# Reading the scores' blocks back from DRAM: four 32-partition reads in place of one with a broadcast outermost dimension

## The chip, the cores and the metric

The kernel runs on one core of one Trainium2 chip. The metric is the device time of one execution in microseconds (us). Before the change the median of three runs is 1072.54 us (1072.24 to 1074.22).

## The reference, cut to what matters

One layer of a decoder trunk on 512 tokens with a model width of 2048. Half of the width is an RWKV-7 group of 16 heads of 64 channels, the other half a causal pooling group; both are gated, concatenated, projected and added to the residual, and a gated embedding and a last norm follow.

```python
h = rms_norm(x, norm_g[i])
z = jnp.einsum('btd,dn->btn', h, w_in[i])          # r, k, v, two loras, gates, pool input
...
kk = (k * k_k[i]).astype(f32).reshape(B, T, N_HEADS, HEAD_SIZE)
kk = kk / jnp.maximum(jnp.linalg.norm(kk, axis=-1, keepdims=True), KK_EPS)
...
def step(S, inp):                                   # the recurrence over 512 tokens
    r_t, w_t, k_t, v_t, kk_t, a_t = inp
    sa = jnp.einsum('bhvk,bhk->bhv', S, -kk_t)
    S = (S * w_t[:, :, None, :]
         + sa[..., None] * (kk_t * a_t)[:, :, None, :]
         + v_t[..., None] * k_t[:, :, None, :])
    y_t = jnp.einsum('bhvk,bhk->bhv', S, r_t)
...
x = x + jnp.einsum('btc,cd->btd', y_mix, w_out[i])
gate = jax.nn.sigmoid(jnp.einsum('btd,de->bte', x, w_pg[i]) + b_pg[i])
x = x + gate * jnp.einsum('btq,qd->btd', p[i], w_ple[i])
```

## The kernel before, in words

**Stages.** The first 60 us load and normalise x and turn it. From there to about 715 us the RWKV heads run, two heads (128 channels) at a time, in eight blocks j = 0 to 7, while the large projections of `w_in` fill the gaps on TensorE. The rest are the output projection and the gate (`acc_o`, `acc_g`). All large products are done in three float32 parts: `mm3` (L167) multiplies the high part of the weights by the high and low part of the activations, and the low part by the high one.

**Weights.** `wsplit` (L127) loads a 256 KB chunk (`raw`, issued by SP), makes its rounded part on ScalarE (`whi`, L132) and the rest on VectorE (`wlo`, L133). Each of `raw`, `whi` and `wlo` has four buffers, so a chunk's `whi` can only be made when TensorE has finished with the chunk four before it, and a `raw` load is issued when the `wlo` four before it is made.

**A block.** The recurrence is done in chunks of 64 tokens. `prepare` makes the scaled keys and queries; `scores` (L646) multiplies them on TensorE (`pm`), masks the products into `mt` on VectorE (L661), writes the 32x32 diagonal parts to DRAM as `nd` (L677, four writes), and reads them back (L682) into two tiles `n_0` and `n_1` of 128 partitions (the name `n` in the trace), in which each of four groups of 32 partitions holds the same copy. `invert` (L702) inverts the small triangular blocks in 31 steps on VectorE, two instructions each: `tm` (L709), then `xw` (L713). The first 16 steps read `n_0`, the other 15 `n_1`. The result goes to DRAM (`xd`, L717) and back (`x1`, L724; its name in the trace is `x`), and `gather` (L730) turns it (`y`, L777), multiplies it on TensorE (`pq`) and prepares the next recurrence.

**The recurrence.** `recur(j)` (L812) goes through eight chunks: TensorE `py`, VectorE `zs` (L844), TensorE `pu`, ScalarE copies of `pu` (L858), TensorE `ps`, VectorE `sbd` (L874). Between these steps `pump` puts groups of matmuls of the large projections (`zg`, `zk`, `zr`, `zv`, `zb`). The inversion of block j+1 is done during the recurrence of block j, and so are the first steps on the keys of block j+2: `prepare_key` (L559) squares the key on ScalarE into `kk` (L562), splits it into `kqh` (ScalarE, L140) and `kql` (VectorE, L141); `norm_key` (L568) sums both with two matmuls named `pss` on TensorE, at a fixed place after the fifth chunk. The tile `kk` has the same buffer as `n_0`.

**What sets the order.** From the RWKV stage on (`pin`, L348) TensorE keeps the order of the program. On the other engines and on the queue of SP, a scheduler puts the instructions into a fixed order when the kernel is built, by its own estimate of durations; `issue_after` and `high_priority` move some of them. On the chip each engine then takes its instructions strictly in that order, so an instruction that waits holds up all that stand behind it on the same engine.

Of the kernel before, what the change touches and what calls it, by code (L numbers as in the profile page):

```python
# [34 lines left out]
def trunk_kernel(ctx: ExitStack, tc: tile.TileContext, x, p, norm_g, w_in, mu, w0, w_up, a0, a_up,  # L35
                 k_k, k_a, r_k, ln_w, ln_b, w_pool, pool_scale, w_out, w_ple, w_pg, b_pg, final_g, out):
    nc = tc.nc
    PSUM = bass.MemoryType.PSUM
    x, p, w_in, w_out, w_ple, w_pg = x[0], p[0, 0], w_in[0], w_out[0], w_ple[0], w_pg[0]
    out = out[0]  # L40
# [118 lines left out]
    def mm(*a, **k):  # L159
        i = nc.tensor.matmul(*a, **k)  # L160
        return tc.keep_in_program_order(i) if pin[0] else i
# [34 lines left out]
    n_ = 0  # L196
# [13 lines left out]
    for kind, nm, j in jobs:  # L210
# [7 lines left out]
        else:  # L218
            g, i = j // 4, j % 2
# [79 lines left out]
    for d in range(KT):  # L299
        xt_half(0, d)  # L300
        if d in WPOS:
            c = len(wl_)
# [18 lines left out]
    for g, win in enumerate(WINDOWS):  # L321
        t_ = cst.tile([P, win], F32, name=f"rc{g}")
# [28 lines left out]
    def load_ab(j):  # L351
        jc = slice(j * P, (j + 1) * P)
        w2 = []
        for nm, src in (("u", w_up), ("a", a_up)):
            raw = rw.tile([P, P], F32, name=f"{nm}r{j}", tag=f"l{nm}r")
            for h in range(2):
                nc.sync.dma_start(out=raw[64 * h:64 * h + 64, :], in_=src[0, :, jc])
            w2.append((raw, rw.tile([P, P], F32R, name=f"{nm}s{j}", tag=f"l{nm}s")))
        wab[j] = w2
# [24 lines left out]
    for nm, rows in (("u", slice(0, 64)), ("a", slice(64, 128))):  # L384
# [3 lines left out]
        t_ = rw.tile([P, T], F32R, name=f"{nm}hh")  # L388
# [257 lines left out]
    def scores(j):  # L646
        ar, bk, v_ = (st_[j][n_] for n_ in ("ar", "bk", "v_"))
        kph, kpl = st_[j].pop("kp")

        mt = rw.tile([P, 2, 8, 2, C], F32, name=f"mt{j}", tag="mt", bufs=2)  # L650
        pm = [[psM.tile([P, T], F32, name=f"pm{j}_{par}0", tag="m"),
               psY.tile([P, T], F32, name=f"pm{j}_{par}1", tag="y")] for par in range(2)]
        for par in range(2):
            for q in range(4):
                for h in range(2):
                    rows = slice(64 * h, 64 * h + 64)
                    mm(pm[par][h][:, q * P:(q + 1) * P], bk[rows, q, 2 * par:2 * par + 2, :],
                       ar[rows, q, 2 * par:2 * par + 2, :], start=True, stop=True)
        for par in range(2):
            for h in range(2):  # L660
                nc.vector.tensor_tensor(mt[:, par, h::2, :, :],  # L661
                                        pm[par][h].rearrange("p (u a t) -> p u a t", u=4, a=2),
                                        msk[:, par:par + 2, :].unsqueeze(1).to_broadcast([P, 4, 2, C]), ALU.mult)


        ps = psM.tile([P, T], F32, name=f"pbo{j}", tag="m")
        mm(ps, blk, kph, start=True, stop=False)
        mm(ps, blk, kpl, start=False, stop=True)
        bv = rw.tile([P, T], F32, name=f"bv{j}", tag="bv", bufs=2)
        nc.vector.tensor_tensor(bv, ps, v_, ALU.mult)  # L670

        nd = dram.tile([2, 2, 8, 32, 32], F32, name=f"nd{j}", tag="nd")
        for par in range(2):
            pb = 64 * (1 - par)
            for b in range(2):
                rows = slice(pb + 32 * b, pb + 32 * b + 32)
                nc.sync.dma_start(out=nd[par, b].rearrange("u r c -> r u c"),  # L677
                                  in_=mt[rows, par, :, 1 - par, 32 * b:32 * b + 32])
        nb = []
        for i in range(2):  # L680
            t_ = rw.tile([P, 16, 32], F32, name=f"n32{j}_{i}", tag=("kk", "kp")[i])
            n_ = nc.sync.dma_start(out=t_, in_=nd[:, :, :, 16 * i:16 * i + 16, :].rearrange(  # L682
                "a b u r c -> (a b u) r c").unsqueeze(0).to_broadcast([4, 32, 16, 32]))
            nb.append(t_)
        if j + 1 < NJ:
            with tc.issue_after(n_.ins):
                load_ab(j + 1)
        bg = rw.tile([P, NCH, 4, 32], F32, name=f"bg{j}", tag="bk")
        with tc.issue_after(n_.ins):
            for q in range(4):  # L690
                nc.sync.dma_start(out=bg[32 * q:32 * q + 32],
                                  in_=st_[j]["bkd"].rearrange("(b k) (c q i) -> q k c b i", b=4, q=4, i=32)[q])
        if j:
            vg, vd = vgs[j]
            with tc.issue_after(n_.ins):
                for q in range(4):
                    nc.sync.dma_start(out=vg[32 * q:32 * q + 32],
                                      in_=vd.rearrange("(b k) (c q i) -> q k c b i", b=4, q=4, i=32)[q])
        st_[j].update(mt=mt, nb=nb, bv=bv, bg=bg)
# [260 lines left out]
    prepare(0)  # L960
    pump(H3)
    scores(0)
    pump(H2)
    for _ in invert(0):
# [3 lines left out]
    for j in range(NJ):  # L968
        def between():
            pump(H3 if j + 1 < NJ else HC[2])  # L970
            if j + 1 < NJ:
                scores(j + 1)
                pump_to(H2)

        if j + 1 == NJ:
            pn.append(rw.tile([P, 2, T // 32, 32], F32, name="pn", tag="ar", bufs=2))
            for q in range(4):
                for c in range(2):
                    nc.sync.dma_start(out=pn[0][32 * q:32 * q + 32, c],
                                      in_=p[:, c * P + 32 * q:c * P + 32 * q + 32].rearrange("(b k) i -> k b i", k=32))  # L980
        if j + 1 < NJ:
            prepare(j + 1)
        elif gates:
            gates.pop()()
        recur(j, invert(j + 1) if j + 1 < NJ else iter(()), between)
        if j + 1 < NJ:
            gather(j + 1)
# [86 lines left out]
    for ec in range(D // EC):  # L1074
# [3 lines left out]
        for tt in range(NT):  # L1078
            rows = slice(tt * P, (tt + 1) * P)
            t_ = pp.tile([P, EC], F32, name=f"x2_{ec}_{tt}", tag=("u", "sw")[tt // 2])  # L1080
# [3 lines left out]
                                in_=t_.rearrange("p (c e) -> p c e", e=P))  # L1084
# [204 lines left out]
```

## Time and profile before

| what | value |
|---|---|
| median of 3 runs | 1072.54 us (1072.24 to 1074.22) |
| the profiled execution's own time | 1077.76 us |
| its span, first to last instruction | 1076.0 us |
| granted TensorE clock, mean | 0.997 |
| TensorE (PE) busy | 1047.7 us (97%) |
| VectorE (DVE) busy | 711.7 us (66%) |
| ScalarE (ACT) busy | 435.0 us (40%) |
| DMA, mean over the span | 144 GB/s |
| reads of `nd` (n<-nd) | 16, 256 KB each |

The profile is one execution; times within it are microseconds from its first instruction. The timeline's rows give the start, the length, the engine, the line, the operation with its output and inputs, how many instructions are merged into the row, and in brackets how long the engine had been idle before it and what ended that. The order of the rows on one engine is the order in which it executes them. The view of waits adds such idle times up: total, times, longest. SPq is the queue of SyncE, from which most transfers are issued.

### The profile page before, as it was taken

To read this page: it belongs to the slowest core of one execution; us is meant where nothing else is said; L and a number is where in the kernel's file an instruction comes from. 1 tells how busy PE (TensorE), PEld (TensorE's weight loads), DVE (VectorE), ACT (ScalarE), POOL (GpSimd) and SP (SyncE) were. 2 spreads that over 40 slices of the span, in tenths; PEclk is the share of its full clock that TensorE was granted. 3 is DMA by queue.
4 is the path that set the end of the run, shared out by engine and by line. 5 is a ranking of instruction groups with operands and counts; after the bars stand their busy time and mean duration, and the time that the engine had idled before them with its cause. 6 is when DMAs were issued, how large, how long until landed. Compare 5 with 4: busy or idle time off the path is not lost.

```text
span 1076.0 us, 17131 instructions
## 1 busy us (share of the span) xinstructions
PE 1047.7 (97%) x5912; PEld 864.6 (80%) x5912; DVE 711.7 (66%) x1879; ACT 435.0 (40%) x893; POOL 72.6 (7%) x180
## 2 busy tenths in 40 slices
PE   5999999999999999999999999999999999999996
PEld 4888878888877887888888788888888888888885
DVE  6676968878688689687786977464353344435356
ACT  7633424434334345253443344544232232324337
POOL 2100011010110110101101201000000000000000
PEclk9999999999999999999999999999999999999998
DMA  7434453453443544534544453775747659454534
GB/s 237 110 115 101 135 132 95 130 139 99 143 116 100 160 105 128 128 95 133 132 118 133 112 130 108 225 259 163 183 152 190 163 145 272 129 177 159 173 98 157
DMA packets 272733, 155.41 MB, mean 144 GB/s; under 512 B 114449, under 2 KB 235386, under 8 KB 272646
## 3 DMA queue, kind: packets, MB, share of 16 engines
q1 hardware_dynamic: 244630, 125.74, 42.2%
q10 hardware_dynamic: 28016, 28.58, 8.8%
q8 instruction: 46, 0.75, 0.3%
q14 instruction: 41, 0.34, 0.1%
HBM read 128.79 MB, written 24.95 MB: 143 GB/s over the span
## 4 chain that ended last, share of the span: by engine, by line
PE 81%; DVE 9%; DMA 5%; ACT 2%; issue 2%; SPq 1%; ACTq 0%; DVEq 0%
PE acc_o L160 16%; PE acc_g L160 16%; PE zb L160 10%; PE zv L160 7%; PE zr L160 7%; PE zg L160 6%; PE zk L160 6%; PE py L160 2%; PE pple L160 2%; DMA n<-nd 1%; PE pu L160 1%; PE pm L160 1%; DMA x<-xd 1%; PE pp L160 1%; PE ps L160 1%
## 5 line engine op out<-in xcount | busy, mean ns | idle before, releaser
L133 DVE TENSOR_TENSOR wlo_g<-raw_g,whi_g 128x512 fp32r<-128x512 f32 x84 | 57.1, 687 | 76.0 <-ACT whi_g L132 73.8
L160 PE MATMUL zb<-hhi,whi_b 128*128 128x512 f32 x256 | 105.5, 412 | 0.0
L160 PE MATMUL zb<-hhi,wlo_b 128*128 128x512 f32 x256 | 100.4, 392 | 0.0
L160 PE MATMUL zb<-hlo,whi_b 128*128 128x512 f32 x256 | 99.8, 390 | 0.0
L160 PE MATMUL acc_o<-wlo_o,yhi 128*128 128x512 f32 x256 | 99.6, 389 | 0.0
L160 PE MATMUL acc_o<-whi_o,ylo 128*128 128x512 f32 x256 | 99.6, 389 | 0.0
L133 DVE TENSOR_TENSOR wlo_o<-raw_o,whi_o 128x512 fp32r<-128x512 f32 x64 | 43.9, 690 | 81.0 <-ACT whi_o L132 72.8
L160 PE MATMUL acc_o<-whi_o,yhi 128*128 128x512 f32 x256 | 94.7, 389 | 0.0
L132 ACT CAST whi_g<-raw_g 128x512 fp32r<-128x512 f32 x84 | 51.9, 620 | 103.0 <-PE acc_g L160 57.4
L160 PE MATMUL acc_g<-whi_g,x2hi 128*128 128x512 f32 x208 | 81.1, 390 | 0.0
L160 PE MATMUL acc_g<-wlo_g,x2hi 128*128 128x512 f32 x208 | 81.0, 389 | 0.0
L160 PE MATMUL acc_g<-whi_g,x2lo 128*128 128x512 f32 x208 | 80.7, 390 | 0.0
L881 POOL TENSOR_SCALAR s0p<-sbd,pw 64x64 f32<-64x64 f32 x96 | 56.4, 587 | 336.6 <-DVE sbd L874 245.1
L132 ACT CAST whi_o<-raw_o 128x512 fp32r<-128x512 f32 x64 | 39.5, 621 | 96.1 <-PE acc_o L160 55.0
L132 ACT CAST whi_b<-raw_b 128x512 fp32r<-128x512 f32 x64 | 39.6, 620 | 75.9 <-PE zb L160 22.4
L713 DVE TENSOR_TENSOR xw<-xw,tm 128x60 f32<-128x60 f32 (+24 forms) x248 | 52.2, 210 | 7.1
L160 PEld LDWEIGHTS zb<-hhi,wlo_b 128*128 128x128 f32 x256 | 48.0, 188 | 10.8
L160 PEld LDWEIGHTS acc_o<-whi_o,ylo 128*128 128x128 f32 x256 | 48.1, 188 | 10.1
L160 PEld LDWEIGHTS acc_o<-whi_o,yhi 128*128 128x128 f32 x256 | 48.0, 188 | 10.0
L160 PEld LDWEIGHTS acc_o<-wlo_o,yhi 128*128 128x128 f32 x256 | 48.0, 188 | 9.9
L133 DVE TENSOR_TENSOR wlo_b<-raw_b,whi_b 128x512 fp32r<-128x512 f32 x64 | 43.7, 684 | 17.8 <-ACT whi_b L132 17.2
L160 PEld LDWEIGHTS zb<-hhi,whi_b 128*128 128x128 f32 x256 | 48.2, 188 | 8.6
(289 smaller groups left out, 2502.2 us busy)
## 6 DMA issues: line engine op xcount, KB each, us to landing
raw_b<-in_w_in_dram SPq DMA_DIRECT2D x64, 256.0 KB
raw_o<-in_w_out_dram SPq DMA_DIRECT2D x64, 256.0 KB
raw_g<-in_w_pg_dram SPq DMA_DIRECT2D x64, 256.0 KB
raw_k<-in_w_in_dram SPq DMA_DIRECT2D x32, 256.0 KB
raw_r<-in_w_in_dram SPq DMA_DIRECT2D x32, 256.0 KB
raw_v<-in_w_in_dram SPq DMA_DIRECT2D x32, 256.0 KB
raw_g<-in_w_in_dram SPq DMA_DIRECT2D x32, 256.0 KB
bkd<-bk SPq DMA_DIRECT2D x8, 512.0 KB
```

Of the source, the lines that this page charges most:

```text
L132: made.append(nc.scalar.copy(hi, raw))
L133: made.append(nc.vector.tensor_tensor(lo, raw, hi.bitcast(F32), ALU.subtract))
L160: i = nc.tensor.matmul(*a, **k)
L713: nc.vector.tensor_tensor(xw[:, 0:n_, s + 1:32], xw[:, 0:n_, s + 1:32], tm[:, 0:n_, 0:w_], ALU.add)
L881: nc.gpsimd.tensor_scalar(s0p[hc, :], nxt[hc, hc], pcn[hc], None, ALU.mult)
```

## The change

Each read of `nd` into a tile of 128 partitions was one transfer, whose source has a leading dimension of 4 with step 0 (the broadcast). Now it is four transfers, one into each group of 32 partitions, from the same source without the broadcast. Per block that is eight transfers in place of two, 48 more in the kernel. What is read, where it goes, and all arithmetic stay the same.

```diff
         nb = []
         for i in range(2):
             t_ = rw.tile([P, 16, 32], F32, name=f"n32{j}_{i}", tag=("kk", "kp")[i])
-            n_ = nc.sync.dma_start(out=t_, in_=nd[:, :, :, 16 * i:16 * i + 16, :].rearrange(
-                "a b u r c -> (a b u) r c").unsqueeze(0).to_broadcast([4, 32, 16, 32]))
+            for q in range(4):
+                n_ = nc.sync.dma_start(out=t_[32 * q:32 * q + 32], in_=nd[:, :, :, 16 * i:16 * i + 16, :].rearrange(
+                    "a b u r c -> (a b u) r c"))
             nb.append(t_)
         if j + 1 < NJ:
             with tc.issue_after(n_.ins):
```

From L684 on, line numbers of the changed kernel are one higher. Since the scheduler counts four transfers where it counted one, it also orders VectorE, ScalarE and SP anew. TensorE and GpSimd keep their order. Three places follow, before and after.

SP, the reads of block 3. `raw_r` and `raw_v` are weight loads, `ur` and `ar` small weights of the next block, `bg` another tile read back from DRAM. Before:

```order
L677 DMA nd_3715<-mt_3685 32x8x32 x4
L129 DMA raw_r_2_2113<-in_w_in_dram 128x4x128
L682 DMA n_0_3720<-nd_3715 128x1x512
L682 DMA n_1_3722<-nd_3715 128x1x512
L357 DMA ur_3724<-in_w_up_dram 64x128 x2
L129 DMA raw_r_3_2119<-in_w_in_dram 128x4x128
L357 DMA ar_3728<-in_a_up_dram 64x128 x2
L691 DMA bg_3732<-bkd_3582 32x32x32
```

And now:

```order
L677 DMA nd_3733<-mt_3703 32x8x32 x4
L129 DMA raw_r_2_2125<-in_w_in_dram 128x4x128
L683 DMA n_0_3738<-nd_3733 32x512 x3
L129 DMA raw_r_3_2131<-in_w_in_dram 128x4x128
L683 DMA n_0_3738<-nd_3733 32x512
L683 DMA n_1_3743<-nd_3733 32x512 x2
L129 DMA raw_v_0_2157<-in_w_in_dram 128x4x128
L683 DMA n_1_3743<-nd_3733 32x512 x2
L357 DMA ur_3748<-in_w_up_dram 64x128
```

The fourth read into `n_0` stands behind a weight load, and the small loads of the next block have moved behind all eight reads.

VectorE, the first steps of the inversion of block 3, which is done during the recurrence of block 2 (`sg` belongs to a gate, `i` is an identity). Before:

```order
L874 SCALAR_TENSOR_TENSOR sbd_566<-ps_1_3780,pw_2402,s0p_0_3640 64x64
L377 SCALAR_TENSOR_TENSOR sg_3787<-sg_3787,zg_3614 128x512
L844 TENSOR_TENSOR zs_568<-py_0_3585,mv_3526 64x128
L709 TENSOR_TENSOR tm_3837<-i_116,n_0_3720 128x31
L713 TENSOR_TENSOR xw_3836<-xw_3836,tm_3837 128x31
L709 TENSOR_TENSOR tm_3837<-xw_3836,n_0_3720 128x30
L713 TENSOR_TENSOR xw_3836<-xw_3836,tm_3837 128x30
L133 TENSOR_TENSOR wlo_r_0_2080<-raw_r_0_2077,whi_r_0_2079 128x512
L874 SCALAR_TENSOR_TENSOR sbd_567<-ps_2_3852,pw_2402,s0p_1_3784 64x64
```

And now:

```order
L875 SCALAR_TENSOR_TENSOR sbd_566<-ps_1_3804,pw_2414,s0p_0_3658 64x64
L377 SCALAR_TENSOR_TENSOR sg_3811<-sg_3811,zg_3632 128x512
L845 TENSOR_TENSOR zs_568<-py_0_3603,mv_3544 64x128
L133 TENSOR_TENSOR wlo_r_0_2092<-raw_r_0_2089,whi_r_0_2091 128x512
L710 TENSOR_TENSOR tm_3861<-i_116,n_0_3738 128x31
L714 TENSOR_TENSOR xw_3860<-xw_3860,tm_3861 128x31
L710 TENSOR_TENSOR tm_3861<-xw_3860,n_0_3738 128x30
L714 TENSOR_TENSOR xw_3860<-xw_3860,tm_3861 128x30
L875 SCALAR_TENSOR_TENSOR sbd_567<-ps_2_3876,pw_2414,s0p_1_3808 64x64
```

One weight split has moved from behind the first two steps to ahead of them; the same holds in blocks 0, 1, 5 and 7.

ScalarE and VectorE, the split of the squared key of block 4, which is also done during the recurrence of block 2. ScalarE before:

```order
L562 ACTIVATE kk_4014<-sk_3936,prm 128x512
L140 CAST kqh_4016<-kk_4014 128x512
L132 CAST whi_v_2_2196<-raw_v_2_2194 128x512
L858 COPY uv_3373<-pu_5_4065 64x64 x2
L132 CAST whi_v_3_2202<-raw_v_3_2200 128x512
L372 ACTIVATE sr_4101<-zr_3939,dprm 128x512
L576 COPY kk_4014<-pss_4082 128x512
```

ScalarE now:

```order
L562 ACTIVATE kk_4038<-sk_3960,prm 128x512
L132 CAST whi_v_2_2208<-raw_v_2_2206 128x512
L859 COPY uv_3391<-pu_5_4089 64x64 x2
L132 CAST whi_v_3_2214<-raw_v_3_2212 128x512
L372 ACTIVATE sr_4125<-zr_3963,dprm 128x512
L140 CAST kqh_4040<-kk_4038 128x512
L576 COPY kk_4038<-pss_4106 128x512
```

VectorE before:

```order
L709 TENSOR_TENSOR tm_3837<-xw_3836,n_1_3722 128x5x14
L141 TENSOR_TENSOR kql_4017<-kk_4014,kqh_4016 128x512
L133 TENSOR_TENSOR wlo_v_2_2197<-raw_v_2_2194,whi_v_2_2196 128x512
L713 TENSOR_TENSOR xw_3836<-xw_3836,tm_3837 128x5x14
L709 TENSOR_TENSOR tm_3837<-xw_3836,n_1_3722 128x5x13
L713 TENSOR_TENSOR xw_3836<-xw_3836,tm_3837 128x5x13
L709 TENSOR_TENSOR tm_3837<-xw_3836,n_1_3722 128x5x12
L713 TENSOR_TENSOR xw_3836<-xw_3836,tm_3837 128x5x12
L133 TENSOR_TENSOR wlo_v_3_2203<-raw_v_3_2200,whi_v_3_2202 128x512
L874 SCALAR_TENSOR_TENSOR sbd_566<-ps_5_4090,pw_2402,s0p_4_4007 64x64 x2
```

VectorE now:

```order
L710 TENSOR_TENSOR tm_3861<-xw_3860,n_1_3743 128x5x13
L714 TENSOR_TENSOR xw_3860<-xw_3860,tm_3861 128x5x13
L710 TENSOR_TENSOR tm_3861<-xw_3860,n_1_3743 128x5x12
L714 TENSOR_TENSOR xw_3860<-xw_3860,tm_3861 128x5x12
L133 TENSOR_TENSOR wlo_v_3_2215<-raw_v_3_2212,whi_v_3_2214 128x512
L373 SCALAR_TENSOR_TENSOR sr_4125<-zr_3963,prm,sr_4125 128x511
L141 TENSOR_TENSOR kql_4041<-kk_4038,kqh_4040 128x512
L875 SCALAR_TENSOR_TENSOR sbd_566<-ps_5_4114,pw_2414,s0p_4_4031 64x64 x2
```

`kqh` now stands behind one weight split more on ScalarE and behind `sr`, a step on the projection of r that reads its finished sum; `kql` stands behind the same two on VectorE. In the key splits of blocks 2, 3, 5, 6 and 7 both have likewise moved behind one weight split, without `sr` between that split and them.

## Prediction

> **What bounds the kernel now.** I read the table of engines first, then the view of waits, then the chain of work that ended last, then the timeline of single engines around the places that the change touches. The table of engines has TensorE near its end:
>
> ```profile
> PE 1047.7 (97%) x5912; PEld 864.6 (80%) x5912; DVE 711.7 (66%) x1879; ACT 435.0 (40%) x893; POOL 72.6 (7%) x180
> ```
>
> TensorE is idle for 1076.0 - 1047.7 = 28.3 us in all, its start included. So no change away from TensorE can win more than a few per cent, and one counts only where it removes or makes a gap on TensorE. That TensorE keeps its order makes the gaps easy to follow: each has a place. In the view of waits (total, times, longest) and in the chain (start, length) the read that is changed stands out:
>
> ```profile
> DVE tm L709 <- DMA n<-nd: 22.9, 8, 5.2
> PE py L160 <- DVE sbd L874: 3.1, 4, 1.6
> ```
>
> ```profile
> 287.57 8.56 DMA n<-nd
> 334.93 2.85 DMA raw_g<-in_w_in_dram
> ```
>
> VectorE waits for it in every block, 22.9 us in sum, but TensorE waits for the recurrence's `sbd` only 3.1 us in sum. The read of 256 KB takes 8.56 us from its issue; another load of 256 KB takes 2.85. So the broadcast read is slow, some three times, and most of what it costs VectorE is not on the path. What is, I look up in block 3. SP, then VectorE, then TensorE:
>
> ```profile
> 287.57 1.17 SPq L682 DMA_DIRECT2D n<-nd  x2
> 290.21 0.76 SPq L129 DMA_DIRECT2D raw_r<-in_w_in_dram  x1
> ```
>
> ```profile
> 291.36 0.29 DVE L844 TENSOR_TENSOR zs<-py,mv 64x128 f32<-64x128 f32 x1 [0.31 <-PE py L160]
> 296.16 0.19 DVE L709 TENSOR_TENSOR tm<-i,n 128x31 f32<-128x31 f32 x1 [4.50 <-DMA n<-nd]
> 298.57 0.29 DVE L874 SCALAR_TENSOR_TENSOR sbd<-ps,pw,s0p 64x64 f32<-64x64 f32 x1
> ```
>
> ```profile
> 296.70 0.39 PE L160 MATMUL zk<-hlo,whi_k 128*128 128x512 f32 x1
> 296.93 0.39 PE L160 MATMUL zk<-hhi,wlo_k 128*128 128x512 f32 x1
> 298.92 0.38 PE L160 MATMUL py<-sbd,ar 128*128 128x128 f32 x1 [1.60 <-DVE sbd L874]
> ```
>
> VectorE stands at `tm` for 4.50 us; `sbd` stands behind it in the queue and comes late; TensorE runs out of `zk` and waits for it. In flow one matmul starts 0.23 after the last (296.70 to 296.93), so the gap costs 298.92 - 296.93 - 0.23 = 1.76, which is the idle time in the bracket plus 0.16. Four more gaps in the recurrences have the same form:
>
> ```profile
> 140.26 0.49 PE L160 MATMUL pu<-zs,x 128*128 128x128 f32 x2 [0.84 <-DVE zs L844]
> 152.03 0.49 PE L160 MATMUL py<-sbd,ar 128*128 128x128 f32 x2 [0.70 <-DVE sbd L874]
> 154.32 0.49 PE L160 MATMUL pu<-zs,x 128*128 128x128 f32 x2 [0.40 <-DVE zs L844]
> 591.70 0.49 PE L160 MATMUL py<-sbd,ar 128*128 128x128 f32 x2 [0.55 <-DVE sbd L874]
> ```
>
> With 0.16 each they cost 1.00, 0.86, 0.56 and 0.71. All five make 4.89 us: what the change can give back in the recurrences.
>
> **The change, step 1: the reads.** One issue on SP takes about 0.57 us:
>
> ```profile
> L682 SPq DMA_DIRECT2D n<-nd x16: 517/570/621, 82.9 to 582.0; - x16
> ```
>
> Four issues of 64 KB put the last one 3 x 0.57 = 1.71 after the first, with a weight load between in block 3 (0.76), so it is issued at about 287.57 + 1.71 + 0.76 = 290.0, or some tenths later. If each lands like the 256 KB load above, 2.85 after its issue, `n_0` is whole at about 293; before, it let `tm` go at 296.16. A bound from below is the old rate: a quarter of 8.56 is 2.1 for a quarter of the bytes, which gives 292. The bound from above is 8.56 from the last issue, 298.6: later than before. I take 2.85, since these reads now look like the other loads that fill partitions from DRAM without a broadcast. The Trainium skill, page "DMA: Bandwidth & Descriptors", section "Rules for kernel authors", says that an outermost dimension of size c below 16, such as a leading zero-stride broadcast of c copies, confines the transfer to at most c DMA engines; with the rows 8.56 and 2.85 this agrees, and it would let the new reads land as I take it.
>
> Is that early enough? In block 3 `sbd` needs 298.57 - 296.16 = 2.41 after `tm` is free, and one weight split fewer stands behind `tm` now, about 0.7. With `tm` at 293.3 it comes at 295.0 to 295.7, and TensorE wants it by 296.93 + 0.23 = 297.16. So the whole 1.76 goes. The split moved ahead of `tm` must not wait itself: its `whi_r` starts early enough:
>
> ```profile
> 291.82 0.62 ACT L132 CAST whi_r<-raw_r 128x512 fp32r<-128x512 f32 x1 [1.97 <-PE zk L160]
> ```
>
> It ends at 292.44, before the read lands. The gaps of blocks 1 and 7 are shorter and of the same kind; the one at 140.26, where VectorE is behind with its work, goes if block 0 comes forward (step 3). Step 1: -4.89, and 0 if the reads land no sooner.
>
> **Step 2: the keys.** The new order has a price that the diff does not show. `kqh` and `kql` of the next key now stand behind one weight split more, while their reader `pss` keeps its place on TensorE. The weight splits cannot come early: the high part waits until TensorE frees its buffer. In the key of block 2, ScalarE, VectorE and TensorE:
>
> ```profile
> 166.80 0.60 ACT L132 CAST whi_v<-raw_v 128x512 fp32r<-128x512 f32 x1
> 167.30 0.61 ACT L140 CAST kqh<-kk 128x512 fp32r<-128x512 f32 x1
> 169.10 0.62 ACT L132 CAST whi_v<-raw_v 128x512 fp32r<-128x512 f32 x1 [0.73 <-PE zr L160]
> ```
>
> ```profile
> 167.43 0.69 DVE L133 TENSOR_TENSOR wlo_v<-raw_v,whi_v 128x512 fp32r<-128x512 f32 x1 [0.40 <-ACT whi_v L132]
> 168.04 0.68 DVE L141 TENSOR_TENSOR kql<-kk,kqh 128x512 fp32r<-128x512 f32 x1
> ```
>
> ```profile
> 170.06 0.39 PE L160 MATMUL pss<-kql,blk 128*128 128x512 f32 x1
> 241.25 0.39 PE L160 MATMUL pss<-kql,blk 128*128 128x512 f32 x1
> 315.58 0.39 PE L160 MATMUL pss<-kql,blk 128*128 128x512 f32 x1
> 389.79 0.39 PE L160 MATMUL pss<-kql,blk 128*128 128x512 f32 x1
> 461.75 0.39 PE L160 MATMUL pss<-kql,blk 128*128 128x512 f32 x1
> 534.31 0.39 PE L160 MATMUL pss<-kql,blk 128*128 128x512 f32 x1
> ```
>
> From the start of a `whi` to the end of the `kql` behind it are 168.04 + 0.68 - 166.80 = 1.92 us. Until now the pair stood behind the split of 166.80; now it stands behind that of 169.10, which TensorE releases. So `kql` ends at 171.02, and the `pss` of 170.06 starts 0.96 late. TensorE has nothing else in its queue there. The splits ahead of the pair in the keys of blocks 3, 5, 6 and 7:
>
> ```profile
> 240.29 0.62 ACT L132 CAST whi_v<-raw_v 128x512 fp32r<-128x512 f32 x1 [0.73 <-PE zr L160]
> 388.83 0.62 ACT L132 CAST whi_b<-raw_b 128x512 fp32r<-128x512 f32 x1 [0.58 <-PE zv L160]
> 461.49 0.62 ACT L132 CAST whi_b<-raw_b 128x512 fp32r<-128x512 f32 x1 [0.54 <-PE zv L160]
> 533.35 0.62 ACT L132 CAST whi_b<-raw_b 128x512 fp32r<-128x512 f32 x1 [0.73 <-PE zv L160]
> ```
>
> With 1.92 added they end at 242.21, 390.75, 463.41 and 535.27: late by 0.96, 0.96, 1.66 and 0.96. In the key of block 4 `sr` stands between as well:
>
> ```profile
> 315.96 0.69 ACT L372 ACTIVATE sr<-zr,dprm 128x512 f32<-128x512 f32 x1
> ```
>
> ```profile
> 315.97 0.69 DVE L133 TENSOR_TENSOR wlo_v<-raw_v,whi_v 128x512 fp32r<-128x512 f32 x1 [0.38 <-PE pss L160]
> 317.46 0.75 DVE L373 SCALAR_TENSOR_TENSOR sr<-zr,prm,sr 128x511 f32<-128x511 f32 x1
> ```
>
> The split starts `wlo` at 315.97; about 0.61 later comes `sr` on VectorE, 0.66 later `kql`, which takes 0.68: 317.92 against 315.58, late by 2.34. Step 2 costs 4 x 0.96 + 1.66 + 2.34 = 7.84. Its lower bound is 0, if something ahead lets TensorE arrive later anyway; an upper bound is some 0.1 more for each key's passing of a semaphore, 8.4.
>
> **Step 3: block 0.** Its inversion has no recurrence beside it, so its chain is nearly bare:
>
> ```profile
> 90.77 0.19 DVE L709 TENSOR_TENSOR tm<-i,n 128x31 f32<-128x31 f32 x1 [5.19 <-DMA n<-nd]
> 121.09 0.69 PE L160 MATMUL pq<-y,mt 32*32 32x32 f32 x32 [0.32 <-DVE y L777]
> ```
>
> `n_0` was issued at 82.9 (the row of issues above) and released `tm` at 90.77. By step 1 it would come at about 82.9 + 1.71 + 2.85 = 87.5, some 3 us earlier. But the second `y` on VectorE, for which `pq` waits, now has seven more instructions ahead of it (weight splits and steps on r, k and v), at up to 0.69 each 4.8 us. If the 3 us are kept whole, and VectorE's wait ahead of `y` (some 1.2) takes its part, 4.8 - 3.3 - 1.2 is 0.3 to 0.5 late; if they are lost, up to 3.6; if VectorE does that work in its waits, the gap ahead of `pq` closes, 0.32 + 0.16 = 0.48 gained. I take +0.5, range -0.5 to +3.6.
>
> **Step 4: the rest.** 48 issues more on SP make 27 us of that queue over 500; the loads behind them come at most 6 x 0.57 = 3.4 later per block. Weight loads are issued when a `wlo` is done, three chunks ahead of their use, so I put nothing on it; if that cover is gone, one late chunk per block is some 0.5 us, 4 in all.
>
> **The sum.** -4.89 + 7.84 + 0.5 = +3.45. The profiled execution's own time is 1077.76 (its span 1076.0 and 1.8 around it), so it would be 1081.2 there. That execution is 0.5% above the median of the runs, 1072.54; on the median the same sum gives 1076.0, +0.32%.
>
> **The rivals.**
>
> A, faster: the keys are not late. The place is `pss`; the price is the 7.84; it decides in favour if the `whi` ahead of the pair starts by 170.06 - 1.92 = 168.14 in the key of block 2, 0.96 before the row of 169.10. It would, if TensorE's own wait elsewhere moved `pss` back against its `zr` matmuls. Against it: the `whi` is released by a matmul that stands shortly ahead of `pss` in the same queue, so both move together. For it: a reordering this wide may change which chunk sits there. Time: 1072.54 - 4.89 + 0.5 = 1068.1.
>
> B, no change: half of the keys' price, 3.9, is hidden and the rest cancels with the gains: 1072.54 - 4.89 + 3.9 + 0.5 = 1072.1. For it: `pss` is only two matmuls, and a lateness of 0.96 is little against small shifts of ScalarE's queue.
>
> C, the reads do not come sooner: they pass the DMA engines one behind the other, at the old time, and the gaps stay. Then 1072.54 + 7.84 + 0.5 = 1080.9, with step 3's lost head start up to 1083. Against it stands the row of 2.85. The Trainium skill, page "DMA: Bandwidth & Descriptors", section "Rules for kernel authors", has a rule of this kind too: two transfers to disjoint partition halves are not worth it, since they serialize, and one transfer over 128 partitions is to be used. By that rule the change would do nothing for the reads; no run here shows it, and the rule speaks of a transfer that is not a broadcast.
>
> D, SP falls behind (step 4's lost cover): 1076.0 + 4 = 1080.
>
> **How the numbers follow.** The forecast has 0.57 (own range 1073.5 to 1078.5), A 0.18, B 0.15, C 0.05, D 0.05. A measurement of this kernel tells some 0.2% from no change, 2.1 us: 1070.4 to 1074.7. Faster takes A: 0.18. Same takes B and the lower edge of the forecast's range, 0.07: 0.22. Slower is the rest, 0.60. The range reaches down to A, 1068.0, and up to 1079.5, short of C and D.
>
> **What would show it.** In the profile after: the reads of `nd` land within 3 us of their issue; VectorE's wait for `n` falls from 22.9 to below 10; TensorE's wait for `sbd` falls from 3.1 to below 0.5 (if not, step 1 is wrong). A new row appears among the waits, TensorE `pss` for VectorE's `kql`, six times, about 7 us in sum, the longest over 2 in the key of block 4 (if it is missing or below 3, step 2 is wrong, and the kernel is faster). `pq` of block 0 starts within 1 us of 121.1.

## The result, and the profile after

The changed kernel takes 1082.18 us (median of 5 runs, 1081.75 to 1083.47), the kernel before 1072.83 us (median of 5). The ratio is 1.0088, with a 95% interval of 1.0075 to 1.0102: slower by 0.9%, 9.4 us. The forecast was 1076.0 with a range of 1068.0 to 1079.5. The direction was right; the time lies above the range.

The profiled execution of the changed kernel took 1082.89 us (span 1081.2), close to its median. The first profile of before took 1077.76, 4.9 us above its own median. That difference is the key to what follows.

View of waits, after (total, times, longest):

```profile
PE pss L160 <- ACT kqh L140: 4.0, 6, 1.7
DVE tm L710 <- DMA n<-nd: 2.6, 5, 0.8
PE pss L160 <- DVE kql L141: 2.0, 6, 0.4
PE py L160 <- DVE sbd L875: 0.2, 1, 0.2
```

Two things happened at once. VectorE's wait for the read fell from 22.9 to 2.6 us, and TensorE's wait for `sbd` from 3.1 to 0.2. And a new wait stands on TensorE, six times for `kqh` and six times for `kql`, 6.0 us in sum, which the profile of before does not have at all.

Block 3, the read. SP, VectorE, TensorE after:

```profile
286.60 1.29 SPq L683 DMA_DIRECT2D n<-nd  x3
289.08 0.39 SPq L129 DMA_DIRECT2D raw_r<-in_w_in_dram  x1
289.52 1.43 SPq L683 DMA_DIRECT2D n<-nd  x3
```

```profile
292.45 0.19 DVE L710 TENSOR_TENSOR tm<-i,n 128x31 f32<-128x31 f32 x1 [0.24 <-DMA n<-nd]
295.30 0.29 DVE L875 SCALAR_TENSOR_TENSOR sbd<-ps,pw,s0p 64x64 f32<-64x64 f32 x1
```

```profile
295.97 0.39 PE L160 MATMUL zk<-hhi,wlo_k 128*128 128x512 f32 x1
296.20 0.38 PE L160 MATMUL py<-sbd,ar 128*128 128x128 f32 x2
```

The fourth read into `n_0` is issued at 289.52 and `tm` starts at 292.45, 2.93 after it; `sbd` is done at 295.59, and `py` follows 0.23 after the matmul ahead of it, without a gap. But from the first issue it is 292.45 - 286.60 = 5.85 us: SP needs 2.92 to get the fourth one out, since a weight load stands between.

The key of block 2. ScalarE, VectorE, TensorE after:

```profile
163.26 0.72 ACT L562 ACTIVATE kk<-sk,prm 128x512 f32<-128x512 f32 x1 [1.92 <-issue]
...
166.21 0.62 ACT L132 CAST whi_v<-raw_v 128x512 fp32r<-128x512 f32 x1 [0.73 <-PE zr L160]
166.73 0.61 ACT L140 CAST kqh<-kk 128x512 fp32r<-128x512 f32 x1
```

```profile
166.86 0.69 DVE L133 TENSOR_TENSOR wlo_v<-raw_v,whi_v 128x512 fp32r<-128x512 f32 x1 [0.19 <-ACT whi_v L132]
167.47 0.69 DVE L141 TENSOR_TENSOR kql<-kk,kqh 128x512 fp32r<-128x512 f32 x1
```

```profile
166.70 0.40 PE L160 MATMUL zr<-hhi,wlo_r 128*128 128x512 f32 x1
167.40 0.50 PE L160 MATMUL pss<-kqh,blk 128*128 128x512 f32 x1 [0.30 <-ACT kqh L140]
168.21 0.50 PE L160 MATMUL pss<-kql,blk 128*128 128x512 f32 x1 [0.31 <-DVE kql L141]
168.55 0.38 PE L160 MATMUL ps<-uv,bkn 128*128 128x128 f32 x2
```

The squared key is ready at 163.98; `kqh` starts at 166.73, because the `whi_v` ahead of it waits until 166.21 for TensorE. TensorE itself then stands at `pss`. From the last `zr` to `ps` are 168.55 - 166.70 = 1.85 us. Three steps of 0.23 would be 0.69: that is what the same stretch takes in before, 170.29 - 169.60:

```profile
169.60 0.40 PE L160 MATMUL zr<-hhi,wlo_r 128*128 128x512 f32 x1
170.29 0.38 PE L160 MATMUL ps<-uv,bkn 128*128 128x128 f32 x2
```

So this key costs 1.16 us. The worst is the key of block 4, behind `sr`:

```profile
312.31 0.40 PE L160 MATMUL zr<-hhi,wlo_r 128*128 128x512 f32 x1
314.40 0.51 PE L160 MATMUL pss<-kqh,blk 128*128 128x512 f32 x1 [1.69 <-ACT kqh L140]
315.27 0.75 PE L160 MATMUL pss<-kql,blk 128*128 128x512 f32 x1 [0.37 <-DVE kql L141]
315.82 0.41 PE L160 MATMUL ps<-uv,bkn 128*128 128x128 f32 x1
```

Here it is 3.51, 2.82 more. Read the same way, the keys of blocks 2 to 7 take 1.85, 1.84, 3.51, 1.95, 2.58 and 1.89, in sum 13.62, against 6 x 0.69 = 4.14: 9.5 us. That is the size of the whole loss of 9.4.

One thing comes on top in this execution. Behind the pauses at the key of block 4 TensorE's granted clock fell: its mean from 315 to 320 us is 0.66 (the row is in the last section), which makes 5 x 0.34 = 1.7 us, a small part of it within the 2.82. The mean clock of this execution is 0.996; the other four timed ones have 0.998, so the drop does not show in them.

### The profile page after: what moved, and what is told of

Its sections match the earlier page's. It is cut to its first block, busy times and chain, and to the rows that moved or that the text cites. A ratio compares the mean times of both kernels' runs of the same rounds, so it can differ in the third digit from the quotient of the medians.

```text
span 1081.2 us, 17226 instructions
## 1 busy us (share of the span) xinstructions
PE 1051.2 (97%) x5912; PEld 866.0 (80%) x5912; DVE 712.6 (66%) x1879; ACT 436.4 (40%) x893; POOL 72.5 (7%) x180
```

## The experiments

The theory after this reading (A): the place of the six key splits is the whole loss, and the 4.89 us that step 1 promised did not come because ordinary executions of the kernel before do not have these gaps; they belong to the one execution that was profiled. Rival B: the gaps are always there, and something else in the changed kernel took the gain back. Rival C: the reads themselves, or the added issues on SP, cost the time. The expectations name theory A and these rivals.

**The kernel before, profiled again** (no edit).

> The kernel before, unchanged, profiled and timed once more. The profiled execution of before took 1077.76 us, 4.9 us more than the median of its timed runs, and the five gaps behind the read of nd make 4.89 us. Theory A (the gains of step 1 exist only in that one execution): this profile takes about 1072.8 us and the gaps of 1.76, 0.86, 0.71 and 0.56 us ahead of py and pu in blocks 1, 3 and 7 are gone or below 0.3 us in sum, with VectorE's wait for n well below 22.9 us or placed where it delays nothing. Rival B (the gaps are in every execution, and the changed kernel loses what it gains there by something else): the same gaps, 4 us or more in sum, in an execution of about 1073 us.

It took 1073.16 us (median of 11 runs; before beside it 1073.35, ratio 1.0001, 0.9992 to 1.0010), its profiled execution 1073.06 with a span of 1071.3. Its view of waits, and VectorE and TensorE in block 3:

```profile
DVE tm L709 <- DMA n<-nd: 15.4, 7, 4.5
PE pu L160 <- DVE zs L844: 0.9, 2, 0.8
PE py L160 <- DVE sbd L874: 0.7, 2, 0.5
```

```profile
284.77 1.17 SPq L682 DMA_DIRECT2D n<-nd  x2
```

```profile
290.93 0.19 DVE L709 TENSOR_TENSOR tm<-i,n 128x31 f32<-128x31 f32 x1 [2.07 <-DMA n<-nd]
293.45 0.29 DVE L874 SCALAR_TENSOR_TENSOR sbd<-ps,pw,s0p 64x64 f32<-64x64 f32 x1
```

```profile
294.36 0.38 PE L160 MATMUL py<-sbd,ar 128*128 128x128 f32 x2
```

The same broadcast read landed 290.93 - 284.77 = 6.16 us after its issue, where the first profile had 8.59. `sbd` was done at 293.74, in time for `py` at 294.36, and the gap of 1.76 was not there. Over all blocks TensorE waited 0.7 us for `sbd` instead of 3.1. What is left are about 0.9 ahead of a `pu` in the recurrence of block 0 and about 0.6 ahead of a `py` in that of block 4. So most of what the change was to win is not there to be won in this execution. Rival B falls for this execution; a third profile follows below. What made the read slow in the first profile no run shows.

**The kernel before with the keys late.** The reads stay as they were; edges in the issue order put each key split behind the weight split that it stands behind in the changed kernel:

```diff
+    def behind(a, b):
+        tc.add_manual_dep(a.ins, b.ins.name, mybir.DependencyInfo(
+            mybir.DependencyClass.NoSync, mybir.DependencyReason.DATA), reason="order")
...
         split(kqh, kql, kk)
+        if j >= 2:
+            w = wall[{2: "v2_1", 3: "v3_2", 4: "v4_3", 5: "b4_0", 6: "b5_1", 7: "b6_2"}[j]]
+            behind(smade[0], w[1])
+            behind(smade[1], w[2])
```

`wall` holds each weight chunk's three instructions, `smade` the two of the last split; in the key of block 4 both halves of `sr` are put ahead in the same way.

> The kernel before with its broadcast reads, and only the six key splits moved: kqh behind the weight split that it stands behind in the changed kernel, kql likewise (in the key of block 4 behind sr too). Theory A (the place of the keys is the whole loss): +9.3 us, the six pairs of gaps ahead of pss that the changed kernel shows (1.06, 1.05, 2.5, 1.16, 1.78, 1.10 us), about 1082. Rival C (the reads themselves or the 48 more issues cost it): within 2 us of 1072.8.

It took 1084.31 us; ratio 1.0104, 1.0091 to 1.0117. Its waits:

```profile
PE pss L166 <- ACT kqh L146: 4.3, 6, 1.7
PE pss L166 <- DVE kql L147: 2.0, 6, 0.4
PE py L166 <- DVE sbd L888: 0.9, 2, 0.7
```

The loss is there, and a little more, without a single transfer changed: the place of the keys alone makes it. Rival C falls as the cause of this result. Its median is some 2 us above the changed kernel's. The two profiled executions, which have the same drop of the clock behind the key of block 4, are only 1.0 us apart (1083.87 and 1082.89), and that fits the gaps at `sbd` and `zs` that the broadcast read keeps. For the rest the clock is the likelier cause: all four executions here have a mean of 0.995 or 0.996, four of the changed kernel's five have 0.998. Why the drop came in every execution here is not shown.

**The changed kernel with the keys back.** The same edges the other way round (the weight split behind the key split, in the key of block 4 `sr` as well), and the inversion's steps from the 19th on behind `kql`:

```diff
+            behind(w[1], smade[0])
+            behind(w[2], smade[1])
...
-                with tc.issue_after(lead[0].ins):
+                with tc.issue_after(lead[0].ins), (
+                        tc.issue_after(kmade[j + 2][1].ins) if hop[0] == 16 and j + 2 < NJ else ExitStack()):
```

> The changed kernel with its four reads, and the six key splits held ahead of the weight split behind which the new order put them. Theory A: the gaps ahead of pss go and the time falls to that of the kernel before, 1072 to 1073.5; if the reads also win something in ordinary executions, at most 1 us below. Rival B (a true gain of 4.9 us in the reads): about 1068. Rival C: it stays above 1079.

It took 1072.75 us, before beside it 1073.35; ratio 0.9996, 0.9987 to 1.0004. In its waits there is no row of `pss`:

```profile
DVE tm L723 <- DMA n<-nd: 3.4, 6, 1.0
PE pu L166 <- DVE zs L859: 0.6, 2, 0.4
PE py L166 <- DVE sbd L889: 0.2, 1, 0.2
```

With the keys in place the four reads are neither better nor worse than the broadcast, by what a measurement tells. VectorE's wait for the read falls by 12 us (15.4 to 3.4) and the time does not move: that wait was off the path. Nor does the fall show a faster read, for the new order puts a weight split, with its own wait for ScalarE, where VectorE waited for the read. In block 3 `tm` starts 2.26 us after the `zs` ahead of it here (288.79 to 291.05), 2.37 in the second profile of before (288.56 to 290.93), and 6.06 us after the first issue (284.99) against 6.16. Theory A holds from both sides.

**Two reads of 64 partitions each.**

```diff
-            n_ = nc.sync.dma_start(out=t_, in_=nd[:, :, :, 16 * i:16 * i + 16, :].rearrange(
-                "a b u r c -> (a b u) r c").unsqueeze(0).to_broadcast([4, 32, 16, 32]))
+            for q in range(2):
+                n_ = nc.sync.dma_start(out=t_[64 * q:64 * q + 64], in_=nd[:, :, :, 16 * i:16 * i + 16, :].rearrange(
+                    "a b u r c -> (a b u) r c").unsqueeze(0).to_broadcast([2, 32, 16, 32]))
```

> Two reads for each tile, one into each 64 partitions, each with a broadcast dimension of 2; the order is what the scheduler makes of it, and it leaves the keys of blocks 2, 3, 5, 6 and 7 ahead of the weight split as before, that of block 4 one split later. Theory A: near the kernel before, 1072 to 1075 (only block 4's key may be late, by up to 2 us). Rival C (more issues cost by themselves): half of the loss, about 1077. For the read itself: if the outermost dimension sets how many DMA engines work, each read has two, and n lands no sooner than with the dimension of 4 (tm released 7 to 9 us after the first issue); if not, it lands in between.

It took 1084.15 us (1080.78 to 1087.82); ratio 1.0103, 1.0084 to 1.0123. Theory A's number missed, by another mechanism: no `pss` waits, but the reads come later than with one. The executions also spread with the granted clock, from 1080.78 us at a mean of 0.998 to 1087.82, the profiled one, at 0.993; some 5 us of the profile are the clock (last section).

```profile
DVE tm L710 <- DMA n<-nd: 29.7, 8, 5.9
PE py L160 <- DVE sbd L875: 5.4, 5, 2.3
PE pq L160 <- DVE y L778: 3.2, 4, 1.5
```

```profile
292.82 1.64 SPq L683 DMA_DIRECT2D n<-nd  x3
```

```profile
301.81 0.19 DVE L710 TENSOR_TENSOR tm<-i,n 128x31 f32<-128x31 f32 x1 [5.22 <-DMA n<-nd]
```

In block 3 `n_0` lands 8.99 us after its first issue, against 6.16 to 8.59 in the profiles of before and 5.85 with four reads; over all blocks VectorE waits 29.7 us for it, against 15.4 to 22.9 before. The Trainium skill, page "DMA: Bandwidth & Descriptors", section "Rules for kernel authors", has it that the size of the outermost dimension, when below 16, limits how many DMA engines take part; with a dimension of 2 this trace agrees in direction, though no run here counts the engines. So step 1's mechanism is real when a read lands late enough: here `sbd` is late again and TensorE waits 5.4 us for it.

**Only `n_0` by four reads**, `n_1` as before, nothing held by hand:

```diff
-            for q in range(4):
+            for q in range(4 if i == 0 else 0):
...
+            if i != 0:
+                n_ = nc.sync.dma_start(out=t_, in_=nd[:, :, :, 16 * i:16 * i + 16, :].rearrange(
+                    "a b u r c -> (a b u) r c").unsqueeze(0).to_broadcast([4, 32, 16, 32]))
```

> Only n_0 is read by four transfers, n_1 by one with the broadcast; the order is the scheduler's own, with nothing held by hand. It puts kqh behind uv but ahead of the weight split, and kql behind five more of the inversion's instructions, ahead of the split's low part. Theory A (it is the place behind the split that costs): the waits ahead of pss are at most 0.3 us each, and the time is 1072 to 1075. Rival C (the added reads cost by themselves): half of the 48 issues added, half of the loss, about 1078.

It took 1073.78 us, before beside it 1074.44; ratio 0.9994, 0.9985 to 1.0002. The scheduler left `kqh` ahead of the weight split here, and the waits at `pss` are small, as in the key of block 5:

```profile
384.11 0.40 PE L160 MATMUL pss<-kqh,blk 128*128 128x512 f32 x1
384.63 0.51 PE L160 MATMUL pss<-kql,blk 128*128 128x512 f32 x1
```

`kql` is 384.63 - 384.11 - 0.23 = 0.29 late, as expected at most. Half of the added issues cost nothing that a measurement tells.

**Eight reads of 16 partitions, the keys back.**

```diff
-            for q in range(4):
-                n_ = nc.sync.dma_start(out=t_[32 * q:32 * q + 32], in_=nd[:, :, :, 16 * i:16 * i + 16, :].rearrange(
-                    "a b u r c -> (a b u) r c"))
+            for q in range(8):
+                n_ = nc.sync.dma_start(out=t_[16 * q:16 * q + 16], in_=nd[q % 2, :, :, 16 * i:16 * i + 16, :].rearrange(
+                    "b u r c -> (b u) r c"))
```

> Each tile of n by eight reads of 16 partitions, 112 issues more than the kernel before, the keys held ahead of the split as in the run with four reads and the keys back. If issues on SP cost something, it shows here: eight issues of 0.42 us put n_0's last one some 1.7 us later than with four, with the weight loads between them more. Theory A: n comes later but VectorE or TensorE hides most of it, 1073 to 1076. Rival C: twice the loss of four reads or more, above 1080.

It took 1084.27 us; ratio 1.0096, 1.0081 to 1.0111. Theory A's 1073 to 1076 missed, and rival C's number came. SP in block 0, and the waits:

```profile
80.12 0.78 SPq L696 DMA_DIRECT2D n<-nd  x2
81.81 0.39 SPq L129 DMA_DIRECT2D raw_r<-in_w_in_dram  x1
...
96.20 1.86 SPq L696 DMA_DIRECT2D n<-nd  x2
```

```profile
PE pq L166 <- DVE y L791: 6.3, 6, 2.2
PE pu L166 <- DVE zs L859: 3.5, 5, 1.5
```

Sixteen reads take SP from 80.12 to 98, since weight loads stand between them and each of those waits for its buffer. So rival C has a point from which it is true: with 64 reads and the keys back there is no loss, with 128 there is one of about 10 us, by waits at `pq` and `pu`, not at `pss`. In block 0 `tm` starts at 90.59, 2.26 later than with four reads and the keys back (88.33), and TensorE's pause ahead of `pq` is 2.23 us, where that run has 0.16. The waits at `pq` and `pu` are 7.3 us more than in that run; in the profiled execution some 5 us are the granted clock, which fell to half behind two of these pauses (its mean is 0.993, in all four executions 0.993 to 0.995).

**The kernel before, a third profile** (no edit).

> The kernel before once more, one profile. Theory A: as in the second profile of before, the gaps behind the read of nd in the recurrences' py and pu make less than 2 us, and the time is 1071 to 1075. If they make 4 us and more, the first profile was not the odd one, and the time should be about 1077.

It took 1074.68 us. Block 3:

```profile
285.77 1.17 SPq L682 DMA_DIRECT2D n<-nd  x2
```

```profile
292.84 0.19 DVE L709 TENSOR_TENSOR tm<-i,n 128x31 f32<-128x31 f32 x1 [2.98 <-DMA n<-nd]
```

The read took 7.07 us, between the other two. TensorE's gaps in the recurrences that the broadcast read can explain make about 1.2 us. Three profiles of one kernel give 8.59, 7.07 and 6.16 us for this read in block 3, and 1077.76, 1074.68 and 1073.06 us.

**Only `n_0` by four reads, and the keys back**, the version to which the runs point: the edits of both runs together.

> Only n_0 by four reads, as in the run before that did so, and the key splits held ahead of the weight split and of the inversion's later steps: the version that the runs point to. Theory A: the remaining waits ahead of pss (two of about 0.3 us and some smaller) go, and nothing else changes: 1 to 2 us below the kernel before, which is at the edge of what a measurement tells. If it is no better than the run with n_0 alone (0.6 us below), the read is off the path in ordinary executions and there is nothing to win from it.

It took 1072.74 us, before beside it 1073.28; ratio 0.9993, 0.9984 to 1.0002. The `pss` waits are gone, and it is half a microsecond below before, within what the measurement tells. No version was found that is clearly better than the kernel before.

## Why the prediction was right in sign and wrong in size

**Step 1, the mechanism:** right in how a late read reaches TensorE. The reads land 2.93 us after the last issue (2.85 taken), `tm` starts at 292.45 (293 taken), `sbd` is in time, and all the gaps named but the first are gone. Of the one ahead of `pu` in the recurrence of block 0 about 0.6 remains in the changed kernel's profile. The first profile and the run with two reads show that a late read makes such gaps. That four reads take them away in ordinary executions is not shown: most of the gaps are absent from the second and third profile of before as well, and from the first issue the four reads (5.85 us, and 6.06 with the keys back) are hardly sooner than the broadcast read in the second profile (6.16), since SP needs 2.92 us to get to the fourth. The sign that the prediction named, a wait for `sbd` below 0.5, came with 0.2, but it was 0.7 in the second profile without any change.

**Step 1, the size: this is the step that failed.** The prediction put -4.89 us into the sum, from five gaps of one profiled execution, and carried the sum over to the median: "on the median the same sum gives 1076.0". But the profiled execution was 5.2 us above that median, and the prediction noted this without asking where those 5 us lie. The second profile shows that most of them lie in these very gaps: the read, at the end of its spread, took 8.59 us there and not 6.16. In ordinary executions the gaps that the change removes are of the order of 1 us; with the keys back the time is 0.6 us below before, which is within what a measurement tells (0.9996, 0.9987 to 1.0004). So the gain was taken off a median that does not contain these gaps.

**Step 2, the keys:** right in place, cause and order of sizes, and this was most of the forecast; 7.84 was predicted and 9.5 measured. From the start of `whi` to the end of `kql` it is 167.47 + 0.69 - 166.21 = 1.95 in the trace, 1.92 in the prediction. What was missed is small and comes at each key: `pss` starts 0.05 after `kql` is done (168.16 to 168.21), and behind its stop it takes 0.50 and not 0.39, so that `ps` follows after 0.34 and not 0.23. With the 1.95 that is about 0.2 per key. The key of block 4 came at 2.82 for 2.34; with the keys late the same stretch is 3.29 and not 3.51, since there the clock falls only behind it. The 9.5 is also above the bound of 8.4 that the prediction had put on this step.

**Step 3, block 0:** taken at +0.5; the gap at `pq` of block 0, read as in the prediction, went from 0.48 to some 0.3 in the changed kernel's profile. But the second and the third profile of before do not have that gap, so against those executions it is a loss of about 0.4, near the value taken.

**Step 4, SP:** right at four reads, as the runs with the keys back and with `n_0` alone show; the run with eight shows where that cover ends.

The sum with the measured sizes: +9.5 for the keys, 1 or less back from the reads, 0 to 0.4 for the rest, gives 8.5 to 9.9, and 9.4 was measured. With 0.6 in place of 4.89 the prediction's own sum gives 1072.54 + 7.84 + 0.5 - 0.6 = 1080.3; what is left to 1082.18 is about what step 2 was short of. The rival "the keys are not late" did not occur. The rival that the reads come no sooner expected the gaps to stay, which they did not; in the time from the first issue it was nearly right. Rival D, SP falling behind, came only in the run with eight reads. By the second rule that the prediction takes from the Trainium skill, page "DMA: Bandwidth & Descriptors", section "Rules for kernel authors", two transfers to disjoint partition halves are not worth it, since they serialize. This case agrees in so far as the four reads won no time that a measurement tells (0.9996); whether the reads serialize no run here shows.

## What to carry to other kernels

A change that adds instructions to a queue which a scheduler orders is first of all a change of the order everywhere: compare the new order with the places that the bound engine keeps, and price each instruction that has moved behind one paced by that engine. Before a gain is read off one profile, see how far that execution lies from the median; gaps that make up that difference are not a gain. And a long wait on an engine that is not the bound (here 15 to 23 us) may be worth nothing. A pause of the bound engine can cost more than its length: those of 1.69 and 0.37 us at one key in the changed kernel's profile were followed by 1.7 us of lost clock.

## What was not expected of the hardware

TensorE's granted clock fell to half behind some of its pauses. With two reads it did so behind a pause of 1.48 us at the `pq` of block 0, and again behind one of 2.31 us ahead of a `py` in block 3. The windows for two reads (us, PE busy, weight loads, VectorE, ScalarE, GpSimd, granted clock, DMA share, GB/s):

```profile
123.93 0.69 PE L160 MATMUL pq<-y,mt 32*32 32x32 f32 x30 [1.48 <-DVE y L778]
304.56 0.49 PE L160 MATMUL py<-sbd,ar 128*128 128x128 f32 x2 [2.31 <-DVE sbd L875]
```

```profile
125.00:130.00 5.00, 5.00 (x66) 4.34 (x63) 5.00 (x6) 2.61 (x7) 0.40 (x1) 0.50 0.35 102
130.00:135.00 5.00, 5.00 (x22) 4.04 (x22) 4.03 (x8) 1.55 (x4) 0.00 (x0) 0.85 0.58 207
305.00:310.00 5.00, 5.00 (x18) 4.04 (x17) 2.77 (x12) 1.03 (x3) 0.05 (x1) 0.66 0.67 159
```

And for the changed kernel, behind the pauses of 1.69 and 0.37 us at the key of block 4:

```profile
315.00:320.00 5.00, 4.73 (x16) 3.90 (x17) 1.78 (x8) 0.59 (x1) 0.98 (x2) 0.66 0.51 105
```

At half the clock over 5 us and 0.85 over the next 5 the first one costs about 3 us beside the pause itself; 0.66 over 5 us is 1.7. With eight reads the clock fell behind a pause of 2.23 us at the `pq` of block 0 and behind two that make 2.48 at that of block 7. It did not fall behind the pause of 1.60 us in block 3 of the first profile of before, nor behind one of 1.50 ahead of a `pu` with eight reads. So the length of a pause alone does not decide it: 1.48 was followed by a drop, 1.50 and 1.60 were not. Behind the pauses at `pq` come many small matmuls; whether that matters, and what sets the drop off, was not tried.
